# Four token mixers on one core: a thread weaver with decoupled stages, mixer operations at a priority of their own, and TensorE held to the order of emission

## The chip, the cores and the metric

The program runs on one core of a Trainium2 chip. The metric is device time in microseconds (us) of one execution. The kernel before takes 1378.37 us (median of 3 runs, 1376.46 to 1379.80). The engines are named as in the profile: PE is TensorE (matmul), PEld its weight load, DVE is VectorE, ACT is ScalarE, POOL is GpSimd, SP issues the DMAs.

## The reference

One layer over 2048 tokens of width 1024, in float32:

```
h    = rmsnorm(x) * pre_norm_w
proj = h @ w_in                       # 1024 x 3992, split in four groups
y    = [gated_deltanet(p_gdn),        # 4 heads of 64, chunks of 64 tokens, a triangular solve per chunk
        rwkv7(p_rwkv),                # 4 heads of 64, decayed state with a rank-one correction
        short_conv(p_sc),             # bg * conv3(cg * xv) * silu(z)
        gla(p_gla)]                   # 4 heads, key width 32, value width 64, chunks of 64
x    = x + rmsnorm(y @ w_out) * post_norm_w
```

Gated DeltaNet, RWKV7 and GLA each carry a state from chunk to chunk. The first two need, per chunk and head, the inverse of a 64x64 unit triangular matrix.

## The kernel before

Tokens go in 4 blocks of 512 (`NBLK`, `BL`), a block in 4 tiles of 128 (`TT`). For a block, `proj` multiplies h with one 128-channel tile of `w_in` at a time: weights and h are each split in a high and a low float32r part, so that a tile takes 24 matmuls of 512 columns (high x high, high x low, low x high, over 8 slices of the width) into one of two PSUM banks (`pp`). A function per tile takes the result out (`conv` for Gated DeltaNet, `mix` for RWKV7, and so on); its ACT and DVE operations carry a raised priority (`PRIO` 400), as do the split of the weights and the `hl` parts of the next block's h in `front` (`FPRIO` 400). GLA's value projection is the exception: `proj_v` has h as weights and `w_in` moving, in matmuls of 256 columns, and gives tokens by channels.

The mixers run as threads (Python generators) of one weaver, `weave`: `chains` (the recurrences, the state kept in SBUF), `inverses` (blockwise inversion: `Bb`, `W`, `X`, `Y`, `Yb`), `prepare` (gates, norms, decays, then the matrices of a pair of tiles in `gdn_mats` or `rwkv_mats`), `put` (outputs), `stats` (next block's h), `load_out`. The projections are the main thread. The weaver has a clock of its own: `mm` and `tr` add a planned cost, and a thread that yields a number from `LAT` is ready again that much later. Main runs for `BEAT` (1.5) planned us, which is two pieces of four matmuls, then all ready threads are stepped, again and again, until none is ready. Where neither can go on, the clock jumps. Threads also wait for each other's events: `prepare` begins the matrices of pair n when inverse n-1 is done ("I"), the inverses need the matrices ("B"), the chains the inverses.

That gives the order of emission. The order in which each engine executes is made afterwards, by a scheduler that takes the instructions of each engine by priority and readiness; TensorE's order is its choice too, and differs from the emission.

After the last projection, `out_proj` multiplies the four mixers' outputs (which went through DRAM, `yd`) with `w_out`; its weights are loaded by `load_out` once the last Gated DeltaNet tile is out, and 12 of its 16 token tiles need nothing of the last block.

Lines that the steps below touch: L595 `mmb`, L613 W and L618 X of the inverse, L605 the copy to the block diagonal `Yb`, L620 the transpose; L1005 and L1006 the DeltaNet chain's correction; L1064 and L1037 RWKV7's; L435 `hl` of the next block; L893 to L918 RWKV7's preparation; L1103 the normalised output. All matmuls have line L199, all transposes on TensorE L203.

Of the kernel before, what the change touches and what calls it, by code (L numbers as in the profile page):

```python
# [12 lines left out]
F16 = mybir.dt.float16  # L13
# [32 lines left out]
CST = {"ident": 0, "dlt": 128, "cum": 256, "msi": 384, "rst": 640, "bones": 640 + BL}  # L46
NCST = 640 + BL


def make_consts():  # L50
    c = np.zeros((P, NCST + P), np.float32)
    r = np.arange(P)
    blk = r[:, None] // 64 == r[None, :] // 64
    a, b = r[:, None] % 64, r[None, :] % 64
    c[:, 0:128] = np.eye(P)
    c[:, 128:256] = blk & (a > b)
    c[:, 256:384] = blk & (a <= b)
    j, i = r[:, None] % 64, np.arange(64)[None, :]

    c[:, 384:640] = np.concatenate([i > j, i >= j, i >= j, i > j], 1)  # L60
    c[:, 640:NCST] = np.arange(BL) % 64 > 0
    c[:, NCST:] = blk

    m = [j == i, -((j // 2 == i // 2) & (i % 2 == 1) & (j % 2 == 0)).astype(np.float32)]
    m += [-((j // (2 * s) == i // (2 * s)) & (j % (2 * s) >= s) & (i % (2 * s) < s)).astype(np.float32) for s in LEVELS]
    return c, np.concatenate([x.astype(np.float16) for x in m], 1)


def layout(inp):
# [4 lines left out]
    starts += [GLA0, GLA0 + 128, GLA0 + 512, GLA0 + 640]  # L74
# [5 lines left out]
    wv = w[:, GLA0 + 256:GLA0 + 512].reshape(KT, P, 256).transpose(1, 0, 2).reshape(P, KT * 256)  # L80
# [8 lines left out]
    for nm, key in (("w0", "rwkv_w0"), ("a0", "rwkv_a0"), ("kk", "rwkv_k_k"), ("ka", "rwkv_k_a"), ("rk", "rwkv_r_k"),  # L89
# [13 lines left out]
        "wv": wv,  # L103
# [24 lines left out]
class Ring:  # L128
# [6 lines left out]
    def __call__(self):  # L135
# [11 lines left out]
    "M4": (512, 4), "BKT": (512, 2), "UV": (512, 2),   # L147
    "ru": (256, 2), "lu": (256, 3), "or": (256, 2),  "Yf": (64 * 8, 1), "y": (256, 1),
    "t2": (BL, 4), "gk": (16, 9), "sx": (64, 1), "dr": (16, 1), "kn": (4 * TT, 3), "rB": (256, 1), "sm": (16, 14),

    "lqk": (BL, 2), "lv": (BL, 2), "lk": (128, 1), "lgz": (2 * BL, 1), "ld": (8, 1), "lg": (BL, 2), "n32": (32, 4), "gs": (TT, 2),
# [5 lines left out]
    "kq": (2 * BL, 2), "gv": (BL, 2), "ggz": (2 * BL, 1), "attn": (256, 2), "kT": (256, 4), "vT": (256, 2),  # L157
    "gu": (256, 3), "t1": (256, 3), "og": (256, 2), "gy": (256, 1),
}
RINGS16 = {"Bh": 1, "Bl": 1, "W": 1, "X": 2, "Y": 1}  # L160
# [7 lines left out]

BEAT = 1.5
# [3 lines left out]
LAT = {"gates": 6.0, "ipre": 2.0, "gates2": 1.0, "norms": 3.2, "chan": 0.9, "pool": 1.38, "decay": 2.6, "mats": 2.2, "inv0": 1.0, "inv1": 2.2,  # L173
       "invr": 0.8, "chA": 1.0, "chB": 0.7, "chC": 0.48, "rpre": 5.0, "rchan": 4.5, "gpre": 3.0, "gA": 1.1,
# [14 lines left out]

class K:  # L190
    def __init__(self, tc, a, out):
        self.tc, self.nc, self.a, self.out = tc, tc.nc, a, out
        self.t, self.left, self.ev, self.threads = 0.0, 0.0, {}, []


    def mm(self, out, w, x, **kw):
        n = math.prod(out.shape[1:])
        self.t += max(0.028, n * (1.67e-3 if w.dtype == F32 else 0.42e-3))
        return self.nc.tensor.matmul(out, w, x, **kw)  # L199

    def tr(self, out, x, ident):
        self.t += out.shape[1] * 0.83e-3
        return self.nc.tensor.transpose(out, x, ident)  # L203

    def thread(self, gen, prio):
        self.threads.append([prio, 0.0, None, gen])
# [12 lines left out]
    def step(self, th):  # L219
# [6 lines left out]
        else:  # L226
            th[1] = self.t + y

    def weave(self):
# [3 lines left out]
        while self.threads:  # L233
# [17 lines left out]
    def setup(self, ctx):  # L251
# [29 lines left out]
        self.rst = g("rst", BL)  # L281
        c16 = c.tile([P, 64 * (2 + len(LEVELS))], F16, name="c16")
# [187 lines left out]
    def load_half(self, blk, wi, i):  # L470
# [4 lines left out]
        if wi == "v":  # L475
            wh, wl = (t.rearrange("p (k c) -> p k c", k=2) for t in self.load_parts(blk, (wi, i), self.a["wv"][:, i * BL:(i + 1) * BL]))
            return (wh, self.hh), (wl, self.hh), (wh, self.hl)
# [3 lines left out]
    def proj(self, blk, groups):  # L481
# [3 lines left out]
        for n, (_, tiles, _) in enumerate(groups):  # L485
            nj = range(len(tiles))
            halves = [(n, j, i) for i in range(4 if tiles[0][0] == "v" else 2) for j in nj]
# [8 lines left out]
        for n, j, i, ks in work:  # L496
# [10 lines left out]
            if first:  # L507
                pss[n, j] = self.pp() if tiles[j][0] != "v" else [self.pp() for _ in range(2)]
# [3 lines left out]
            if tiles[j][0] == "v":  # L512
                yield from self.proj_v(ps, i, pairs)
                if i == 3:
                    with self.tc.high_priority(offset=PRIO):
                        tiles[j][1](ps)
                fin += 1
                continue
# [14 lines left out]
            yield 0.0  # L533

    def proj_v(self, ps, i, pairs):

        for q, (w, h) in enumerate(pairs):
            for k in range(2):
                for t in range(TT):
                    o = 256 * (t % 2)  # L540
                    self.mm(ps[t // 2][:, o:o + 256], h[:, 2 * i + k, t * P:(t + 1) * P], w[:, k, :], start=(i + q + k + t % 2 == 0),
                            stop=(i == 3 and q == 2 and k == 1), skip_group_check=True)
            yield 0.0
# [36 lines left out]
    def inverse(self, Bh, Bl, n):  # L580
# [9 lines left out]
        for c in range(2):  # L590
            nc.vector.tensor_copy(Bb[hs(c), :, hs(c)], Bh[hs(c)])
# [6 lines left out]
        nc.vector.tensor_tensor(Y, Bh, m4(self.n1t), ALU.mult)  # L598
        nc.vector.tensor_tensor(Y, Y, I16, ALU.add)
        X = self.R16["X"]()  # L600
        nc.vector.transpose(X, Y)
        def diag():
            Yb = self.Rbd["Yb"]()
            for c in range(2):
                nc.vector.tensor_copy(Yb[hs(c), :, hs(c)], Y[hs(c)])  # L605
# [3 lines left out]
        for lv in range(4):  # L609
# [3 lines left out]
            nc.vector.tensor_tensor(W, v(ps), m4(self.lev[lv]), ALU.mult)  # L613
# [4 lines left out]
            nc.vector.tensor_tensor(X2, v(ps), X, ALU.add)  # L618
            X = X2
            nc.vector.transpose(Y, X)  # L620
# [5 lines left out]
        nc.vector.tensor_tensor(W, v(ps), m4(self.lev[4]), ALU.mult)  # L626
# [8 lines left out]
        nc.vector.tensor_tensor(X2, v(px), X, ALU.add)  # L635
        nc.vector.tensor_tensor(Y, py, Y, ALU.add)
# [3 lines left out]
        nc.vector.tensor_tensor(T, I16, X, ALU.subtract)  # L640
# [8 lines left out]
        nc.vector.tensor_tensor(R, T, v(ps), ALU.subtract)  # L649
# [8 lines left out]
        nc.vector.tensor_tensor(v(Yf), v(ps), Y, ALU.add)  # L658
# [133 lines left out]
    def gdn_mats(self, tt, Bh, Bl):  # L792
# [10 lines left out]
        kT, vT = g["kT"][tt], self.R["vT"]()  # L803
        nc.vector.tensor_tensor(h4(kT), h4(kT), bc(g["ke"]), ALU.mult)
        ps = self.psa()
        for pr in range(2):
            self.tr(ps[:, pr * P:(pr + 1) * P], g["v"][pr][:, tt * P:(tt + 1) * P], self.ident)
        nc.vector.tensor_tensor(h4(vT), h4(ps[:, 0:256]), bc(g["kv"]), ALU.mult)
# [21 lines left out]
        return dict(attn=h4(attn), kT=kT, vT=vT)  # L830
# [38 lines left out]
    def rwkv_prep(self, blk):  # L869
# [10 lines left out]
        for pr in range(2):  # L880
# [15 lines left out]
            nc.scalar.activation(e[:, :, 1:65], c3(G), AF.Exp)  # L896
            ev = e.rearrange("p (a c) t -> p a c t", c=2)
            en, ak = self.t2(), self.t2()
            nc.scalar.activation(en, G, AF.Exp, scale=-1.0)
            kk = self.t2()  # L900
# [4 lines left out]
            nc.vector.tensor_tensor(slot(bks, 0), c4(ak), c4(en), ALU.mult)  # L905
            nc.scalar.activation(av, av, AF.Identity, scale=self.d[:, 17 + pr:18 + pr], bias=self.d[:, 13 + pr:14 + pr])
            nc.vector.tensor_tensor(k_, k_, m3(av), ALU.mult)
            nc.vector.scalar_tensor_tensor(m3(add[:, pr, :]), r_, self.pcol("rk", pr), k_, ALU.mult, ALU.mult)
            nc.vector.tensor_tensor(k_, k_, m3(en), ALU.mult)
# [39 lines left out]
    def rwkv_mats(self, tt, Bh, Bl):  # L949
# [22 lines left out]
        for pr in range(2):  # L972
            bd = BK[pr][:, 2 * tt:2 * tt + 2, :]
# [4 lines left out]
        for cp in range(2):  # L978
            for pr in range(2):
                o = (2 * cp + pr) * P  # L980
                self.tr(ps[:, o:o + P], BK[pr][:, 2 * tt + cp, :], self.ident)
# [478 lines left out]
```

## Time and profile before

| | |
|---|---|
| median of 3 runs | 1378.37 us |
| profiled execution | 1379.89 us, span 1378.1 us |
| TensorE busy | 1284.7 us (93%) |
| VectorE busy | 967.7 us (70%) |
| ScalarE, GpSimd busy | 530.2 us, 355.5 us |
| mean granted TensorE clock | 0.985 |
| DMA | 204.63 MB, mean 148 GB/s |

The chain of waits that ended last is TensorE almost throughout, so time is read from TensorE: what it executes, and where it stood still and for whom. The wait view gives for each waiting engine the operation that released it, total us, times, and the longest; the stretch view gives busy us of every engine in stretches of 50 us with the granted clock.

### The profile page before, as it was taken

The numbers are of one execution on the slowest core, as the hardware profiler recorded it, in microseconds if no ns is written. First come the engines' busy times: TensorE is split into PE (matmuls) and PEld (weight loads), VectorE is DVE, ScalarE is ACT, GpSimd is POOL, SyncE is SP. The second block draws the span as 40 slices with busy tenths as digits, with TensorE's granted clock in tenths as the row PEclk, the third lists the DMA queues.
The fourth block names the chain that finished last, engine by engine and source line by source line (L and its number), as shares of the span: only waits on it lengthen the run. The fifth ranks groups of instructions, "written<-read, shape, count | busy, mean of one in ns | idle before, by whom it ended". The sixth has DMA issues, their size and how long they took to land. (4 is left out here: it accounts for less than half of the span.)

```text
span 1378.1 us, 26007 instructions
## 1 busy us (share of the span) xinstructions
PE 1284.7 (93%) x10088; PEld 982.1 (71%) x10088; DVE 967.7 (70%) x2194; ACT 530.2 (38%) x1167; POOL 355.5 (26%) x437
## 2 busy tenths in 40 slices
PE   5989988899999999999999999999998998999997
PEld 3767766767667767767777677776776776677886
DVE  5766698869876895778657977888669847743232
ACT  4663454336242431425423432453224325133221
POOL 5554444201221021101301210203111135233321
PEclk9999999999999999999999999999999999999999
DMA  8776554544244424453543335432444363233442
GB/s 283 263 258 231 206 177 146 177 152 133 82 139 146 157 89 135 146 177 105 173 146 130 130 120 174 144 110 68 127 143 145 103 198 121 89 99 116 151 151 100
DMA packets 98509, 204.63 MB, mean 148 GB/s; under 512 B 9153, under 2 KB 39249, under 8 KB 98385
## 3 DMA queue, kind: packets, MB, share of 16 engines
q1 hardware_dynamic: 98384, 202.96, 44.6%
q8 instruction: 79, 1.29, 0.4%
q14 instruction: 46, 0.37, 0.1%
HBM read 153.65 MB, written 49.28 MB: 147 GB/s over the span
## 5 line engine op out<-in xcount | busy, mean ns | idle before, releaser
L199 PE MATMUL pp<-hh,w 128*128 128x512 f32 (+1 forms) x2144 | 609.6, 408 | 7.6 <-DMA w<-parts 5.9
L199 PEld LDWEIGHTS pp<-hh,w 128*128 128x128 f32 (+1 forms) x2144 | 389.8, 190 | 92.0 <-issue 4.7
L199 PE MATMUL pp<-hl,w 128*128 128x512 f32 (+1 forms) x1088 | 323.1, 408 | 2.0 <-POOL hl L435 2.0
L199 PEld LDWEIGHTS pp<-hl,w 128*128 128x128 f32 (+1 forms) x1088 | 198.2, 190 | 45.4 <-POOL hl L435 3.8
L352 POOL TENSOR_TENSOR w<-raw,w 128x512 fp32r<-128x512 f32 (+1 forms) x102 | 129.3, 1270 | 223.6 <-ACT w L351 143.0
L351 ACT CAST w<-raw 128x512 fp32r<-128x512 f32 (+1 forms) x102 | 60.3, 593 | 130.5 <-issue 56.8
L356 POOL TENSOR_TENSOR sm<-sm,mhalf 128x4 f32<-128x4 f32 (+1 forms) x64 | 59.3, 927 | 193.4 <-DVE sm L1099 148.7
L199 PE MATMUL pp<-woh,w 128*128 128x512 f32 x256 | 71.8, 401 | 0.0
L681 DVE SCALAR_TENSOR_TENSOR pq<-pq,par,pq 128x512 f32<-128x512 f32 x72 | 59.4, 826 | 11.0 <-ACT pq L678 8.5
L605 DVE COPY Yb<-Y 64x512 f16<-64x512 f16 x160 | 55.8, 349 | 2.2
L199 PEld LDWEIGHTS <-Yb 128*128 128x128 f16 x640 | 25.2, 98 | 41.5 <-issue 22.9
L199 PEld LDWEIGHTS pp<-woh,w 128*128 128x128 f32 x256 | 47.6, 191 | 9.7
L199 PE MATMUL psi<-W,Yb 128*128 128x64 f16 x640 | 32.7, 194 | 22.3 <-DVE W L613 17.5
L618 DVE TENSOR_TENSOR X<-psi,X 128x512 f16<-128x512 f32 x64 | 43.9, 686 | 12.8 <-PE psi L199 12.5
L199 PEld LDWEIGHTS <-Bb 128*128 128x128 f16 x768 | 29.8, 99 | 29.5 <-issue 23.4
L613 DVE TENSOR_TENSOR W<-psi,c 128x512 f16<-128x512 f32 x64 | 43.8, 685 | 5.9 <-PE psi L199 5.3
L1393 DVE SCALAR_TENSOR_TENSOR pq<-pq,sm,x 128x512 f32<-128x512 f32 x32 | 24.6, 769 | 30.4 <-DMA x<-in_x 19.7
L620 DVE STREAM_TRANSPOSE Y<-X 128x512 f16<-128x512 f16 x64 | 45.2, 707 | 0.7
L199 PE MATMUL psi<-X,Bb 128*128 128x64 f16 x768 | 40.0, 195 | 6.2 <-DVE X L618 4.2
L1382 ACT ACTIVATE x<-pp 128x512 f32<-128x512 f32 x32 | 19.1, 598 | 64.1 <-PE pp L199 64.1
L847 ACT COPY pq<-pp 128x512 f32<-128x512 f32 x36 | 21.1, 586 | 53.0 <-PE pp L199 53.0
L199 PE MATMUL pp<-w,hh 128*128 128x256 f32 x256 | 36.6, 289 | 0.1
(320 smaller groups left out, 2152.4 us busy)
## 6 DMA issues: line engine op xcount, KB each, us to landing
w<-parts SPq DMA_DIRECT2D x174, 512.0 KB, 3.3
parts<-w SPq DMA_DIRECT2D x58, 512.0 KB, 4.0
raw<-in_wt SPq DMA_DIRECT2D x58, 256.0 KB, 3.2
x<-in_x SPq DMA_DIRECT2D x56, 256.0 KB, 3.0
raw<-yd SPq DMA_DIRECT2D x32, 256.0 KB, 2.9
out<-pq SPq DMA_DIRECT2D x32, 256.0 KB, 2.0
x<-in_xt SPq DMA_DIRECT2D x24, 256.0 KB, 2.9
w<-parts_v SPq DMA_DIRECT2D x12, 512.0 KB, 3.3
```

The costliest lines, as they stand in the source:

```text
L199: return self.nc.tensor.matmul(out, w, x, **kw)
L351: self.nc.scalar.copy(hi, src)
L352: self.nc.gpsimd.tensor_tensor(lo, src, hi.bitcast(F32), ALU.subtract)
L356: self.nc.gpsimd.tensor_tensor(dst, x, self.mhalf[:, 0:x.shape[1]], ALU.pow)
L605: nc.vector.tensor_copy(Yb[hs(c), :, hs(c)], Y[hs(c)])
L613: nc.vector.tensor_tensor(W, v(ps), m4(self.lev[lv]), ALU.mult)
L618: nc.vector.tensor_tensor(X2, v(ps), X, ALU.add)
L620: nc.vector.transpose(Y, X)
L681: nc.vector.scalar_tensor_tensor(acc, p[:, i:i + BL], self.pcol("conv", 4 * ct + i), acc, ALU.mult, ALU.add)
L847: nc.scalar.copy(p[:, 1:], ps)
L1382: nc.scalar.activation(junk, ps[i], AF.Square, accum_out=ss[:, i:i + 1])
L1393: nc.vector.scalar_tensor_tensor(o, o, r, x, ALU.mult, ALU.add)
```

## The change

Six things change together.

1. **One step per visit.** A thread that yields a positive number is stepped once in a visit; before, a visit went on until no thread was ready.
2. **Order held.** `mm` and `tr` tie each TensorE instruction to the one emitted before it, so TensorE executes in the order of emission.
3. **Priority.** The inverse's and the chains' operations on DVE and ACT go through wrappers (`self.uv`, `self.ua`) at a priority of 800 (`URGENT`), above the 400 of the projections.
4. **Decoupled stages.** `prepare` may be two pairs ahead of the inverses (`Bh` and `Bl` get two buffers, `M4` six, `attn` three). `gdn_mats` and `rwkv_mats` give up what the inverse doesn't need to `gdn_more` and `rwkv_more`, which run after the matrices; the chains wait for them ("M").
5. **Preparations in pieces.** `rwkv_prep` and `gla_prep` yield two or three times more (`rpre` 5.0 becomes 1.0 and three `burst` of 0.5). To pay for the buffers, `rwkv_prep` reuses `add` and `lw` (`t2` 4 to 3), `BKT` goes (the transposes are copied back into `BK`), `gy` is merged with `y`, `rst` becomes float16.
6. **v by channel.** GLA's v is projected like every other tile, in two tiles, and each token tile's v is transposed on TensorE in `gla` and copied out together with `ke`.

```diff
 class K:
     def mm(self, out, w, x, **kw):
         n = math.prod(out.shape[1:])
         self.t += max(0.028, n * (1.67e-3 if w.dtype == F32 else 0.42e-3))
-        return self.nc.tensor.matmul(out, w, x, **kw)
+        return self.after(self.nc.tensor.matmul(out, w, x, **kw))
...
+    def after(self, ins):
+        if self.prev is not None:
+            info = mybir.DependencyInfo(mybir.DependencyClass.NoSync, mybir.DependencyReason.DATA)
+            self.tc.add_manual_dep(ins.ins, self.prev.ins.name, info, reason="order of emission")
+        self.prev = ins
+        return ins
...
+class Urgent:
+    def __getattr__(self, name):
+        op = getattr(self.eng, name)
+        def f(*a, **kw):
+            with self.tc.high_priority(offset=URGENT):
+                return op(*a, **kw)
+        return f
...
             elif ready:
+                self.visit += 1
                 while ready:
                     for th in ready:
                         self.step(th)
-                    ready = [th for th in self.threads if th[0] < 99 and self.can(th)]
+                    ready = [th for th in self.threads if th[0] < 99 and self.can(th) and th[4] < self.visit]
...
-        todo += [(None, (("v", fv),), None)]
+        ... for i, t in enumerate([qf, kf] + v)]
...
-            nc.vector.tensor_tensor(W, v(ps), m4(self.lev[lv]), ALU.mult)
+            self.uv.tensor_tensor(W, v(ps), m4(self.lev[lv]), ALU.mult)
...
-                    if n:
-                        yield "I", n - 1
+                    if n > 1:
+                        yield "I", n - 2
...
+                    self.done("B", n, lat=LAT["mats"])
+                    for i in range(2):
                         if pair:
                             yield "T", name, blk, i
-                        m = yield from (self.gdn_mats if name == "G" else self.rwkv_mats)(...)
-                        ms.append(m)
-                    self.mats[n] = ms, B
-                    self.done("B", n, lat=LAT["mats"])
+                        yield from more(2 * pair + i, ms[i])
+                    self.done("M", n, lat=LAT["more"])
...
-        self.tr(pt[:, 0:P], L["ed"][:, ts], self.ident)
-        nc.scalar.copy(ke, pt[:, 0:P])
+        for i, t in enumerate([L["ed"]] + L["v"]):
+            self.tr(pt[:, i * P:(i + 1) * P], t[:, ts], self.ident)
+        self.ua.copy(kv, pt[:, 0:3 * P])
```

The order in which the instructions stand changes at these places. First VectorE at the end of the first block, where the next block's `hl` is made while an inverse runs. Before:

```order
L605 COPY Yb_153<-Y_150 64x8x64 x2
L435 TENSOR_TENSOR hl<-x_143,hh 128x512
L435 TENSOR_TENSOR hl<-x_144,hh 128x512
L613 TENSOR_TENSOR W_147<-psi,c_203 128x512
L428 SCALAR_TENSOR_TENSOR x_143<-x_143,par,E_71 128x512
L618 TENSOR_TENSOR X_148<-psi,X_149 128x512
```

And now (L201 is the wrapper's line, L463 the line of `hl`):

```order
L201 COPY Yb_153<-Y_151 64x8x64 x2
L201 TENSOR_TENSOR Sr<-Sr,dr_102 128x256
L201 TENSOR_TENSOR W_148<-psi,c_204 128x512
L456 SCALAR_TENSOR_TENSOR x_142<-x_142,par,E_71 128x512
L571 SCALAR_TENSOR_TENSOR lgz_126<-pq_137,pq_136 128x512
L201 TENSOR_TENSOR UV_79<-psc,kn_105 64x2x64
L201 TENSOR_TENSOR UV_79<-psc,kn_104 64x2x64
L201 TENSOR_TENSOR X_150<-psi,X_149 128x512
L463 TENSOR_TENSOR hl<-x_142,hh 128x512
```

W stood behind two `hl` operations; now the inverse and a chain stand together, and `hl` behind them. From the first to the last of the eight `hl` there are 30, 41 and 26 rows at the three block ends before, and 54, 45 and 45 now.

Next TensorE at the end of the projections, where the last inverse (psi) meets the first matmuls with `w_out` (woh, wol). Before, with repeated rows left out:

```order
L199 MATMUL psi<-X_149,Bb_151 128x64
...
L199 MATMUL pp<-hh,w_159 128x512 x4
...
L199 MATMUL psi<-W_147,Yb_153 128x64
...
L199 MATMUL pp<-hl,w_159 128x512 x4
L199 MATMUL pp<-hh,w_159 128x512
...
L199 MATMUL psi<-X_148,Bb_151 128x64
...
L199 MATMUL pp<-hh,w_159 128x512 x3
L199 MATMUL pp<-hh,w_160 128x512 x3
```

And now:

```order
L215 MATMUL psi<-W_148,Yb_154 128x64
...
L215 MATMUL psi<-X_149,Bb_152 128x64
...
L215 MATMUL psi<-W_148,Yb_153 128x64
...
L215 MATMUL psi<-X_150,Bb_152 128x64
...
L215 MATMUL psi<-W_148,Yb_154 128x64
...
L215 MATMUL psa<-Y_151,W_148 64x64
...
L219 MATMUL psa<-cst,or_86 128x128 x2
...
L215 MATMUL pp<-woh,w_160 128x512 x4
```

Before, some matmuls of a projection stood between any two steps of the inverse; now two levels follow each other with nothing between, and soon after them seven steps of RWKV7's chain with next to nothing. Elsewhere it is the other way round: counted over the whole order, between a step of an inverse or of a DeltaNet or RWKV7 chain and the step whose result it takes there were fewer than 8 projection matmuls of 512 columns (or as many columns in smaller ones) in 117 of 377 places before, and are in 15 of 365 now, 12 of these with none at all. The projections' matmuls (w_in and w_out) stood in 448 unbroken groups and stand in 364.

## Rows read from the trace of the kernel before

**Rows 1.** The page: busy time of each engine, share of the span, instructions.

```profile
PE 1284.7 (93%) x10088; PEld 982.1 (71%) x10088; DVE 967.7 (70%) x2194; ACT 530.2 (38%) x1167; POOL 355.5 (26%) x437
```

**Rows 2.** PE's waits: line, releaser: total us, times, longest us.

```profile
PE psi L199 <- DVE W L613: 17.5, 17, 4.8
PE psa L203 <- POOL gs L356: 11.5, 1, 11.5
PE psc L199 <- DVE gu L1006: 8.2, 16, 1.2
...
PE psi L199 <- DVE X L618: 4.2, 5, 2.1
...
PE psa L203 <- DVE or L1103: 4.0, 3, 3.0
PE psa L199 <- DVE t L801: 3.5, 1, 3.5
PE psi L199 <- DVE Yb L605: 2.5, 4, 0.9
PE psc L199 <- DVE Sg L1037: 2.4, 6, 0.9
...
PE psi L199 <- DVE W L626: 2.1, 3, 1.0
...
PE psa L203 <- ACT t L901: 0.2, 1, 0.2
```

**Rows 3.** Timeline, DVE, 180 to 189 us: start, us, what.

```profile
182.60 2.77 DVE L605 COPY Yb<-Y 64x512 f16<-64x512 f16 x2
...
186.00 1.22 DVE L893 TENSOR_TENSOR_SCAN t<-cst,t 128x512 f32<-128x512 f32 x1
187.15 0.68 DVE L613 TENSOR_TENSOR W<-psi,c 128x512 f16<-128x512 f32 x1
```

**Rows 4.** Timeline, PE, 178 to 189 us.

```profile
187.88 0.58 PE L199 MATMUL psi<-W,Yb 128*128 128x64 f16 x8 [4.78 <-DVE W L613]
```

**Rows 5.** Timeline, DVE and then PE, 262 to 266 us.

```profile
262.55 2.27 DVE L435 TENSOR_TENSOR hl<-x,hh 128x512 fp32r<-128x512 f32 x2
...
265.47 0.39 PE L199 MATMUL psi<-W,Yb 128*128 128x64 f16 x8 [0.87 <-DVE W L613]
```

**Rows 6.** Stretches: PE, PEld, DVE, ACT, POOL busy, PEclk, DMA share, GB/s.

```profile
50.00:100.00 50.00, 44.68 (x221) 35.42 (x220) 36.46 (x82) 33.11 (x74) 26.08 (x29) 0.90 0.72 249
150.00:200.00 50.00, 44.66 (x286) 33.51 (x285) 41.54 (x80) 25.01 (x46) 25.38 (x24) 0.93 0.51 180
450.00:500.00 50.00, 46.76 (x359) 35.48 (x358) 46.05 (x98) 27.09 (x53) 8.98 (x11) 1.00 0.39 125
1150.00:1200.00 50.00, 43.99 (x375) 31.84 (x375) 38.19 (x73) 16.23 (x36) 20.05 (x18) 0.97 0.32 102
```

**Rows 7.** Chain that ended last: start us, us, what.

```profile
1217.18 2.05 PE pp L199 x8
...
1220.07 1.85 PE pp L199 x8
...
1273.60 97.06 PE pp L199 x428
```

**Rows 8.** PE's groups: busy us, mean ns, then idle before.

```profile
L199 PE MATMUL pp<-hh,w 128*128 128x512 f32 (+1 forms) x2144 | 609.6, 408 | 7.6 <-DMA w<-parts 5.9 <-ACT hh L434 1.6
...
L199 PE MATMUL pp<-w,hh 128*128 128x256 f32 x256 | 36.6, 289 | 0.1
...
L199 PE MATMUL pp<-w,hl 128*128 128x256 f32 x128 | 18.6, 288 | 0.0
...
L203 PE MATMUL psa<-cst,rv 128*128 128x128 f32 x32 | 7.0, 280 | 0.3 <-DVE M L964 0.3
```

**Rows 9.** DVE's groups of the inverse.

```profile
L605 DVE COPY Yb<-Y 64x512 f16<-64x512 f16 x160 | 55.8, 349 | 2.2
L620 DVE STREAM_TRANSPOSE Y<-X 128x512 f16<-128x512 f16 x64 | 45.2, 707 | 0.7
...
L613 DVE TENSOR_TENSOR W<-psi,c 128x512 f16<-128x512 f32 x64 | 43.8, 685 | 5.9 <-PE psi L199 5.3
```

More of the change, by code (lines that the diff above doesn't have):

```diff
@@ L73, in layout @@
     starts += [SC0 + P * i for i in range(8)]
-    starts += [GLA0, GLA0 + 128, GLA0 + 512, GLA0 + 640]
+    starts += [GLA0 + P * i for i in range(6)]
     tiles = [w[:, s:s + P].reshape(KT, P, P).transpose(1, 0, 2).reshape(P, KT * P) for s in starts]
@@ L167 @@
 FPRIO = 400
+URGENT = 800
 BEAT = 1.5
@@ L227, in step @@
             th[1] = self.t + y
+            if y > 0.0:
+                th[4] = self.visit
     def weave(self):
@@ L486, in proj @@
             nj = range(len(tiles))
-            halves = [(n, j, i) for i in range(4 if tiles[0][0] == "v" else 2) for j in nj]
+            halves = [(n, j, i) for i in range(2) for j in nj]
             order += halves
@@ L507, in proj @@
             if first:
-                pss[n, j] = self.pp() if tiles[j][0] != "v" else [self.pp() for _ in range(2)]
+                pss[n, j] = self.pp()
             if n == 0:
@@ L829, in gdn_mats, with gdn_more @@
         nc.gpsimd.tensor_tensor(Bl, h4(B32), Bh, ALU.subtract)
-        return dict(attn=h4(attn), kT=kT, vT=vT)
+        return dict(attn=h4(attn))
+    def gdn_more(self, tt, m):
+        nc = self.nc
+        g = self.g
+        bc = lambda s: s[:, 4 * tt:4 * tt + 4].unsqueeze(2).to_broadcast([P, 4, 64])
+        kT, vT = g["kT"][tt], self.R["vT"]()
+        nc.vector.tensor_tensor(h4(kT), h4(kT), bc(g["ke"]), ALU.mult)
+        ps = self.psa()
+        for pr in range(2):
+            self.tr(ps[:, pr * P:(pr + 1) * P], g["v"][pr][:, tt * P:(tt + 1) * P], self.ident)
+        nc.vector.tensor_tensor(h4(vT), h4(ps[:, 0:256]), bc(g["kv"]), ALU.mult)
+        m.update(kT=kT, vT=vT)
+        yield 0.0
     def rwkv_proj(self):
@@ L971, in rwkv_mats, with rwkv_more @@
         nc.gpsimd.tensor_tensor(Bl, h4(B32), Bh, ALU.subtract)
-        for pr in range(2):
-            bd = BK[pr][:, 2 * tt:2 * tt + 2, :]
+        yield 0.0
+        return dict(M4=M4)
+    def rwkv_more(self, tt, m):
+        nc = self.nc
+        r = self.r
+        BK = r["BK"]
+        bds = [BK[pr][:, 2 * tt:2 * tt + 2, :] for pr in range(2)]
+        for pr, bd in enumerate(bds):
             for c in range(2):
@@ L977, in rwkv_mats @@
         ps = self.psa()
[L978 to L981, printed above, removed]
-        bt = self.R["BKT"]()
-        nc.scalar.copy(bt, ps)
+        for pr, bd in enumerate(bds):
+            for cp in range(2):
+                o = (2 * pr + cp) * P
+                self.tr(ps[:, o:o + P], bd[:, cp], self.ident)
+        for pr, bd in enumerate(bds):
+            nc.scalar.copy(bd, ps[:, 2 * P * pr:2 * P * pr + 2 * P].rearrange("p (c x) -> p c x", c=2))
         ps = self.psa()
@@ L1145, in prepare @@
                 for pair in range(TT // 2):
-                    if n:
-                        yield "I", n - 1
+                    if n > 1:
+                        yield "I", n - 2
                     B, ms = [self.R16[x]() for x in ("Bh", "Bl")], []
+                    mats, more = (self.gdn_mats, self.gdn_more) if name == "G" else (self.rwkv_mats, self.rwkv_more)
+                    for i in range(2):
+                        tt = 2 * pair + i
+                        if tt == 3:
+                            yield "T", name, blk, 0
+                        m = yield from mats(tt, *(t[:, 4 * i:4 * i + 4, :] for t in B))
+                        ms.append(m)
+                    self.mats[n] = ms, B
+                    self.done("B", n, lat=LAT["mats"])
                     for i in range(2):
@@ L1313, in gla @@
         o = u1()
-        nc.scalar.copy(o, po[:, 0:256])
+        self.ua.copy(o, po[:, 0:256])
         self.norm(o, u1, EPS, False)
```

143 lines of the change are left out of this document (60 added, 83 removed).

## The prediction

> **What bounds the kernel now.** First the page's busy times: TensorE works 1284.7 of a span of 1378.1 us, VectorE 967.7 [rows 1]. So TensorE sets the pace, 93.4 us of the span have no matmul in them, and VectorE is the engine on which the rest hangs. What TensorE has to compute hardly changes; the question is how much of the 93.4 us goes, and what the new order loses elsewhere.
>
> Second, TensorE's waits. 11.5 us are the wait for the first norm, at the start, which the change doesn't touch. The mixers' waits are what it aims at: 17.5 for the inverse's W, 8.2 for DeltaNet's correction, 4.2, 4.0, 3.5, 2.5 and 2.4, together 42.3, and 18 smaller entries from 2.1 down to 0.2, together 17.1 [rows 2]. That makes 59.4 us, nearly all behind VectorE. What remains of the 93.4 is the end after the last matmul, waits for weights, h and gates.
>
> Third, why W is late. The longest wait, 4.78 us, stands at 187.9 [rows 4]. On VectorE, W itself takes 0.68; ahead of it went two copies drawn out to 2.77 and an RWKV7 scan of 1.22, which no inverse waits for [rows 3]. At the first block end two `hl` operations take 2.27 us right ahead of W, and TensorE waits 0.87 [rows 5]. So the waits are VectorE's queue order more than its total. Only more: in some stretches VectorE is busy 46.05 of 50 us while TensorE has 46.76 [rows 6]. There a better order moves a wait rather than removes it.
>
> Fourth, the granted clock. Most stretches have 1.00, but 50 to 100 us has 0.90 and 150 to 200 has 0.93 [rows 6]; the second contains the 4.78 us wait [rows 4], and 1150 to 1200, one of six stretches at 0.97, has TensorE idle for 6.0 us [rows 6]. [...]
>
> [...]
>
> **The change, part by part**, against the profiled execution's 1379.9 us (span 1378.1 and 1.8 outside it).
>
> *One step per visit, and order held.* Now all but 15 of 365 steps have 8 projection matmuls or more ahead of them, 1.85 us or 2.05 [rows 7], where 117 of 377 had fewer. W needs 0.685, X and the transpose about 0.7 each [rows 9], so 1.85 us hide one of them and one foreign operation of some 0.8. *Priority* puts W right behind its own copies rather than behind `hl` or a scan. Bounds: nothing of the 59.4 us goes (VectorE's total is unchanged, and busy stretches stay busy), or all of it. The waits inside 1150 to 1200, 6.0 us of the 50 [rows 6], I treat below, which leaves 53.4. I take 60%: most waits have one or two foreign operations as their cause, as rows 3 and 5 show, but the stretches with VectorE at 46 of 50 keep theirs. **-32.**
>
> *Fewer breaks.* 364 groups of projection matmuls instead of 448. Eight matmuls take 2.05 us behind a group of small mixer matmuls and 1.85 behind a transpose [rows 7]; at the rate of the long unbroken run, 97.06 / 428 x 8, they take 1.81. A break costs 0.04 to 0.24 us, 84 fewer give 3 to 20. I take 0.12: **-10.**
>
> *Clock.* [...] If three fifths of the waits go, some of the drops stay, and the gates' and start's waits aren't touched: **-6.**
>
> *v by channel.* Out: 36.6 + 18.6 = 55.2 us of 256-column matmuls [rows 8]. In: 8 tiles of 24, 192 x 609.6/2144 = 54.6. Also in: 32 transposes of 128 columns for v, for which RWKV7's 32 took 7.0 us busy [rows 8]; they stand behind another transpose of the same group, so less of them may show. The copy out grows from 128 to 384 columns on ScalarE, which has 848 us free. **+5** (bounds +3 and +7).
>
> *The end of the projections.* In the held order the last inverse's two levels have nothing between their steps. A level on VectorE is X, transpose, two copies, W: 0.69 + 0.71 + 0.70 + 0.69 = 2.8 us [rows 9], of which TensorE fills 0.8 with its own two steps of 0.4: 2 x 2.0 = 4. Then three more operations of 0.7 for the closing step, 2, and some five uncovered steps of RWKV7's chain, not less than half of a W each and not more than a whole one, 1.7 to 3.5. Sum 7.7 to 9.5. The same place loses 6.0 us now [rows 6]: **+3** (bounds +1 and +12, the upper one if the first weights of `w_out` come late as well).
>
> *The block ends.* `hl` now lies behind the mixers' operations: from first to last there are 144 rows on VectorE at three block ends instead of 97. At the mean of 967.7/2194 = 0.44 us [rows 1], 47 rows are 21 us by which the next block's h is finished later. TensorE has mixers' steps of its own there and needs the first slices first: **+5** (bounds 0 and +21).
>
> *Decoupling and pieces.* Same instructions; earlier matrices let an inverse run beside the chain of the pair before, so the mixers' steps come in common groups (the 84 breaks fewer). It also packs more of VectorE's work into the same time; that is the upper bound of the first part. Only three `t2` instead of four tie the two halves of `rwkv_prep` closer together; nothing on TensorE waits for them now beyond 0.2 us, by the last row of the waits [rows 2]. 0.
>
> Sum: -32 -10 -6 +5 +3 +5 = -35. 1379.9 - 35 = 1344.9 profiled; the median shown lies 1.5 lower, which gives **1343 us**. The remaining uncertainty of the first term alone, 40 to 85% of 53.4, is 1330 to 1354; with the others, the likeliest case's own range is 1320 to 1364.
>
> **Rivals.**
>
> *All waits go.* If priority and spacing empty the whole list: -53 -17 -14 +3 +1 +0 = -80, so 1298. For it: nearly every wait names VectorE, and VectorE has 410 us free over the span. Against it: 46 of 50 busy where the mixers overlap.
>
> *VectorE is the bound.* Where inverse and chain run side by side, a level (2.8 us) and the chain's operations compete with the projections' own 0.8 us operations, and TensorE waits for PSUM or `hl` instead of for W. Then a quarter of the waits goes: -13 -10 -2 +5 +3 +10 = -7, 1371. For it: rows 6, third row. Against it: the average, 70%.
>
> *Slower: a late operand now stops everything.* TensorE can't be given another order by the scheduler any more, and VectorE executes its own in the order given, an urgent operation that waits for a matmul holding back the projections' results behind it. Place: the three block ends and the end of the projections. Price: 21 + 12 + 7 for transposes, and the rest of the waits only changes its place, with 10 us won and the breaks' saving of 3: +27, 1405. It decides once less than about 40 us is won by the first three parts together, so already from a third of the mixers' waits.
>
> [...]
>
> *The order does nothing.* That the waits come from VectorE's total and neither priority nor spacing matters, while the costs above are small: within 0.2%. That is the narrow strip between the two rivals before.
>
> **Chances.** Forecast 0.54; all waits go 0.12; VectorE the bound 0.16; slower 0.14; nothing 0.04. The range of 8 in 10 runs from 1302 to 1384: it holds the forecast, most of the second case and of the third, and cuts half of the slower one. 0.2% is 2.8 us, about what a measurement of this kernel can tell from no change, so faster means below 1375.6. Forecast, all waits, and three quarters of the third case are faster: 0.78. Within: 0.06. Slower: 0.16.
>
> **What the profile after would show.** The wait for W falls from 17.5 to below 7, that for DeltaNet's correction from 8.2 to below 2; VectorE's busy time stays at 960 to 975 and its share rises to 72%; TensorE's busy time rises or falls by no more than 15 us; one cluster of waits of 8 to 12 us appears around the first w_out matmuls, with psi and psc steps in it; at the block ends waits of pp for `hl` appear, of 2 us each or less; the granted clock is 0.99. Wrong would be: waits of pp for ScalarE or VectorE that sum to over 20 us, a wait for W still above 12, or a busy TensorE below 1260, which would mean that much of what counts as busy is waiting.

## The result and the profile after

The changed kernel takes 1464.19 us (median of 4 runs, 1462.09 to 1465.25), the kernel before 1377.41 us beside it (1370.01 to 1379.80): a ratio of 1.063, 95% interval [1.0605, 1.0657]. The forecast was 1343 and faster.

The profiled execution has a span of 1461.4 us, 83.3 more than before. The page, busy time by engine:

```profile
PE 1306.4 (89%) x9928; PEld 994.6 (68%) x9928; DVE 972.3 (67%) x2194; ACT 532.4 (36%) x1181; POOL 357.4 (24%) x437
```

Against [rows 1], VectorE, ScalarE and GpSimd do what they did, to 5 us. TensorE is busy 21.7 us longer and idle 1461.4 - 1306.4 = 155.0 us instead of 93.4, so 61.6 of the 83.3 us are idle time. Who it waits for (line, releaser: total us, times, longest; L201 is the wrapper's line):

```profile
PE psc L215 <- DVE gu L201: 17.6, 18, 2.2
PE psa L215 <- DVE t L809: 15.1, 5, 3.7
PE psi L215 <- DVE X L201: 14.0, 8, 4.5
PE psa L219 <- POOL gs L384: 12.1, 1, 12.1
PE psi L215 <- DVE W L201: 9.1, 18, 1.8
PE pp L215 <- ACT hh L462: 8.7, 8, 2.8
PE psa L215 <- DVE AR L928: 8.6, 4, 2.4
PE psa L215 <- DVE sm L1117: 7.4, 2, 3.7
PE psa L219 <- DVE attn L829: 7.1, 8, 4.4
PE psa L215 <- DVE M L982: 6.9, 4, 2.2
PE psa L215 <- DVE gk L736: 6.2, 2, 3.9
```

W, the first row of [rows 2], fell from 17.5 to 9.1. Instead the correction (`gu`) rose from 8.2 to 17.6, `t` of DeltaNet's matrices from 3.5 to 15.1, and steps stand in the list that had no entry or a small one: the gates' product (`sm`, `gk`), RWKV7's `AR` and `M`, DeltaNet's `attn`. The 7.4 us under `sm` belong to the gates' product as well (its operand is `gk`; the profile names the VectorE operation that ended last, one of the outputs' norm), which had 4.0 us before. The waits are spread over many operands, not held by one.

Two of these places, PE's timeline (start us, us, what, [idle before <-releaser]):

```profile
364.64 1.08 PE L215 MATMUL pp<-hh,w 128*128 128x512 f32 x4
365.65 0.45 PE L215 MATMUL psc<-ru,Yf 64*64 64x64 f32 x8
369.98 1.35 PE L215 MATMUL psa<-gk,cst 128*128 128x16 f32 x6 [3.88 <-DVE gk L736]
...
371.93 2.08 PE L215 MATMUL pp<-hh,w 128*128 128x512 f32 x4
...
525.00 2.07 PE L215 MATMUL psa<-AR,BK 64*128 64x128 f32 x14 [2.39 <-DVE AR L928]
529.25 2.07 PE L215 MATMUL psa<-AR,BK 64*128 64x128 f32 x14 [2.18 <-DVE M L982]
```

At 366 TensorE stands for 3.88 us before the gates' product of the next tiles, though the projection matmuls behind it need nothing from it: they are executed right after it. Then four of them take 2.08 us where four took 1.08 just before: the granted clock is 1.00 through the wait, 0.51 in 370 to 372 us and 0.50 in 372 to 376, and these four matmuls alone add 1.00 us to the 3.88 of the wait. The stretches that answer to [rows 6]:

```profile
50.00:100.00 50.00, 41.73 (x212) 32.82 (x211) 36.33 (x80) 33.03 (x74) 27.92 (x31) 0.90 0.71 243
...
500.00:550.00 50.00, 43.07 (x330) 33.41 (x329) 46.42 (x99) 24.30 (x52) 10.11 (x10) 0.90 0.32 102
...
1200.00:1250.00 50.00, 34.33 (x329) 26.59 (x328) 38.54 (x69) 19.75 (x43) 27.48 (x23) 0.84 0.46 145
```

Only 6 of the first 26 stretches have 1.00, where 18 had before. The clock records of both traces have two values, 1.00 and 0.50 (24 records of each after, 10 of each before), so the time at the lower one is 2 x (1 - mean clock) x span: 2 x 0.049 x 1461.4 = 143 us after, 2 x 0.015 x 1378.1 = 41 before. If matmuls at 0.50 last twice as long, an estimate from the 2.08 and 1.08 us above, the extra 102 us would have been 51 at the least at 1.00, had all of it been matmuls; part of it was waiting, so 51 is an upper bound of the clock's share. TensorE's busy time grew by 21.7 us, less than that.

### The profile page after: what moved, and what is told of

Read it like the earlier page. It is cut to its first block, busy times and chain, and to the rows that moved or that the text cites. A ratio compares the mean times of both kernels' runs of the same rounds, so it can differ in the third digit from the quotient of the medians.

```text
span 1461.4 us, 25697 instructions
## 1 busy us (share of the span) xinstructions
PE 1306.4 (89%) x9928; PEld 994.6 (68%) x9928; DVE 972.3 (67%) x2194; ACT 532.4 (36%) x1181; POOL 357.4 (24%) x437
## 4 chain that ended last, share of the span: by engine, by line
PE 54%; DVE 30%; issue 5%; DMA 4%; ACT 3%; POOL 3%; SPq 0%; ACTq 0%; POOLq 0%; DVEq 0%
PE pp L215 40%; PE psc L215 6%; PE psa L215 4%; DVE gu L201 3%; DVE Y L201 2%; PE psi L215 2%; DVE X L201 2%; DVE Yb L201 2%; PE psa L219 2%; DVE W L201 2%; POOL sm L384 1%; DVE Sg L201 1%; DMA x<-in_xt 1%; DVE pq L689 1%; DVE x L456 1%
## 5 line engine op out<-in xcount | busy, mean ns | idle before, releaser
L215 PE MATMUL pp<-hh,w 128*128 128x512 f32 (+1 forms) x2272 | 644.3, 414 | 10.7 <-ACT hh L462 8.7
L215 PEld LDWEIGHTS pp<-hh,w 128*128 128x128 f32 (+1 forms) x2272 | 423.9, 194 | 106.1 <-ACT hh L462 10.1
L215 PE MATMUL pp<-hl,w 128*128 128x512 f32 (+1 forms) x1152 | 339.1, 411 | 2.7 <-POOL hl L463 1.5
L215 PEld LDWEIGHTS pp<-hl,w 128*128 128x128 f32 (+1 forms) x1152 | 211.8, 192 | 51.2 <-DVE hl L463 3.8
L384 POOL TENSOR_TENSOR sm<-sm,mhalf 128x4 f32<-128x4 f32 (+1 forms) x64 | 61.6, 962 | 258.5 <-DVE sm L1124 234.9
L201 DVE TENSOR_TENSOR W<-psi,c 128x512 f16<-128x512 f32 x80 | 54.8, 685 | 15.4 <-PE psi L215 14.2
L201 DVE TENSOR_TENSOR X<-psi,X 128x512 f16<-128x512 f32 x80 | 54.9, 686 | 10.8 <-PE psi L215 10.2
L201 DVE COPY Yb<-Y 64x512 f16<-64x512 f16 x160 | 56.5, 353 | 1.8
L863 ACT COPY pq<-pp 128x512 f32<-128x512 f32 x36 | 21.2, 588 | 94.0 <-PE pp L215 94.0
L215 PE MATMUL psa<-AR,BK 64*128 64x128 f32 x256 | 31.2, 357 | 19.1 <-DVE AR L928 8.6
L1426 DVE SCALAR_TENSOR_TENSOR pq<-pq,sm,x 128x512 f32<-128x512 f32 x32 | 24.1, 755 | 34.2 <-DMA x<-in_x 23.6
L201 DVE STREAM_TRANSPOSE Y<-X 128x512 f16<-128x512 f16 x64 | 45.0, 703 | 0.4
L215 PEld LDWEIGHTS psa<-AR,BK 64*128 64x128 f32 x256 | 25.5, 248 | 25.3 <-DVE AR L928 9.5
```

The source lines that it names most:

```text
L201: return op(*a, **kw)
L215: return self.after(self.nc.tensor.matmul(out, w, x, **kw))
L384: self.nc.gpsimd.tensor_tensor(dst, x, self.mhalf[:, 0:x.shape[1]], ALU.pow)
L863: nc.scalar.copy(p[:, 1:], ps)
L1426: nc.vector.scalar_tensor_tensor(o, o, r, x, ALU.mult, ALU.add)
```

## The experiments

### The order held, alone and taken away

To the kernel before only the tie is added (`o_hold`); from the changed one only the tie is taken (`u_hold`).

```diff
-        return self.nc.tensor.matmul(out, w, x, **kw)              # o_hold; tr in the same way
+        return self.after(self.nc.tensor.matmul(out, w, x, **kw))
...
-        if self.prev is not None:                                  # u_hold
+        if False:
```

> The kernel before with TensorE tied to the order of emission and nothing else. Theory A (the held order is the greater part of the loss by itself): 1420 to 1450 us, TensorE idle 125 to 150 us, clock 0.95 to 0.965. Rival (the held order only hurts together with the new emission, its burst of matrices and its early preparations): 1370 to 1400.

> The changed kernel with the tie between TensorE's instructions taken out; emission, priorities and everything else as changed. Theory A (the held order is the cost: TensorE stops at each operand that is later than the planner thought, and nothing may be moved into the gap): 1340 to 1400 us, TensorE's waits down from 155 us idle to below 110. Theory B (the priority of 800 starves the preparations that TensorE needs next): little change, 1440 to 1470, since the same operations on VectorE are still put last. Theory C (the emission itself is bad: matrices are emitted too soon after their preparation and four at once for three banks): 1400 to 1440, the scheduler repairs a part.

`o_hold`: 1461.82 us, ratio 1.0628 [1.0578, 1.0678], clock 0.950. `u_hold`: 1403.12, 1.0187 [1.0134, 1.024], clock 0.979. So the tie on the old kernel makes the whole loss, 85 us, where 1420 to 1450 was expected; the five other edits, on top of the tie, make none (1464 against 1462), and without it they still cost 25 us. `u_hold` lies just above the range of theory A (the order) and within that of theory C (the emission): taking the tie out wins back 61 us, not all. In `o_hold` TensorE executes the same 10088 matmuls as before: it is busy 1307.2 us instead of 1284.7 and idle 153.9 instead of 93.4, so 60.5 of the 83.0 us by which the span grew are idle time. The waits in `o_hold` (its lines are 7 higher than before's):

```profile
PE psi L199 <- DVE W L620: 44.3, 24, 5.4
PE psa L203 <- POOL gs L363: 12.8, 1, 12.8
PE psc L199 <- DVE UV L1071: 12.7, 12, 1.9
PE psc L199 <- DVE gu L1013: 11.7, 12, 1.8
```

The wait for W is 44.3 us where it was 17.5 [rows 2]. The gates' place of above in `u_hold`:

```profile
356.10 0.45 PE L215 MATMUL psc<-ru,Yf 64*64 64x64 f32 x8
356.48 1.19 PE L215 MATMUL pp<-hh,w 128*128 128x512 f32 x4
357.52 1.08 PE L215 MATMUL pp<-hl,w 128*128 128x512 f32 x4
358.52 0.45 PE L215 MATMUL psc<-UV,BK 128*64 128x64 f32 x8
358.81 0.64 PE L215 MATMUL psc<-UV,M 128*64 128x64 f32 x16
359.37 1.66 PE L215 MATMUL pp<-hh,w 128*128 128x512 f32 x6
361.38 0.84 PE L215 MATMUL psa<-gk,cst 128*128 128x16 f32 x6 [0.34 <-DVE gk L736]
```

After the same `ru` product, fourteen projection matmuls and two steps of the chain now stand ahead of the gates' product, and the wait is 0.34 instead of 3.88.

### Which freedom the tie takes

Three weaker ties on the kernel before. In `o_two` projection matmuls (main thread) are tied to each other and the mixers' instructions to each other, with nothing between the two chains. `o_mafter` adds: no mixer step ahead of a projection matmul emitted before it. `o_pafter` adds the reverse: no projection matmul ahead of a mixer step emitted before it.

```diff
+        tie(self.last[self.main])
+        if not self.main:          # o_mafter; o_pafter: if self.main: tie(self.last[False])
+            tie(self.last[True])
```

> The kernel before with the order held in two chains: every projection matmul behind the projection matmul emitted before it, every other TensorE instruction behind the other one emitted before it, with no tie from one chain to the other. Theory A (the loss of the held order is that the scheduler can no longer move projection matmuls against the mixers' steps): the two chains stay free against each other, so 1370 to 1390, wait for W below 15. Theory B (the order of the mixers' steps among themselves is what costs): 1440 to 1465.

> As two chains, and each mixer instruction is also tied behind the last projection matmul emitted before it: projections may be drawn ahead of a mixer's step, the step never ahead of them. Theory A1 (a step whose operand is late is passed by later projection matmuls): 1370 to 1395, as with two chains. Theory A2 (the scheduler gains by taking a ready step earlier than emitted): 1430 to 1465.

> As two chains, and each projection matmul is also tied behind the last mixer instruction emitted before it: a mixer's step may be drawn ahead, projections may not pass a step that waits. Theory A1 (a late step must be passed): nearly all of the loss, 1440 to 1465, wait for W above 30. Theory A2: 1370 to 1400.

| | us | ratio | idle | clock |
|---|---|---|---|---|
| `o_two` | 1382.15 | 1.0035 [1.001, 1.006] | 102.9 | 0.983 |
| `o_mafter` | 1381.42 | 1.0028 [0.9997, 1.006] | 107.2 | 0.983 |
| `o_pafter` | 1458.46 | 1.0582 [1.0519, 1.0645] | 151.6 | 0.954 |
| `o_hold` | 1461.82 | 1.0628 [1.0578, 1.0678] | 153.9 | 0.950 |

(Idle is span minus TensorE's busy time in the profiled execution.) The order of the mixers' steps among themselves and their being drawn ahead of projections are worth some 4 us together (`o_mafter`, whose interval includes no change); as it carries at least as many ties as `o_hold`, the ties themselves aren't what costs. What carries is one direction: a projection matmul that is ready may pass a mixer step that isn't. Theory A1 holds, with nearly the whole loss in `o_pafter`. (Only W's wait was higher than expected in `o_two`, 23.3 us where under 15 was expected.) The clearest place is RWKV7's chain in the first block end. PE's timeline in `o_mafter`:

```profile
369.13 0.63 PE L199 MATMUL pp<-hh,w 128*128 128x512 f32 x2
370.05 0.45 PE L199 MATMUL psc<-ru,Yf 64*64 64x64 f32 x8 [0.29 <-ACT ru L1067]
370.43 1.43 PE L199 MATMUL pp<-hh,w 128*128 128x512 f32 x5
373.52 0.45 PE L199 MATMUL psc<-UV,BKT 128*64 128x64 f32 x8 [1.66 <-DVE UV L1075]
```

and in `o_pafter`:

```profile
374.72 0.69 PE L199 MATMUL psc<-ru,Yf 64*64 64x64 f32 x8
377.28 0.70 PE L199 MATMUL psc<-UV,BKT 128*64 128x64 f32 x8 [1.87 <-DVE UV L1075]
...
386.53 1.23 PE L199 MATMUL psc<-Sr,AR 128*128 128x128 f32 x4 [2.38 <-DVE Sr L1048]
388.22 0.69 PE L199 MATMUL psc<-ru,Yf 64*64 64x64 f32 x8 [0.46 <-ACT ru L1067]
```

The old weaver steps the chain again and again until none is ready, so it emits it in one piece. Where projections may pass, they lie between the steps; where they may not, the chain runs alone, waits at nearly every step, and the same eight `ru` matmuls take 0.69 us instead of 0.45: the page of `o_pafter` has a granted clock of 0.7 in its slice from 364 to 400 us, where that of `o_mafter` has 0.9 or more from 346 to 380.

### More planned distance

If late operands are the loss, later steps might cure it. `LAT` for the steps of the inverse and the chain's first step is raised to 2.7 us, nearly the 2.8 that a level takes on VectorE [rows 9], in `o_hold` (`o_hold_lat`) and in the changed kernel (`u_lat`).

```diff
-"inv0": 1.0, "inv1": 2.2, ... "chA": 1.0
+"inv0": 2.7, "inv1": 2.7, ... "chA": 2.7
```

> The kernel before with the held order, and with longer planned times for the handovers that wait most there: inv0 1.0 to 2.7, inv1 2.2 to 2.7, chA 1.0 to 2.7, so that the planner puts 16 instead of 8 matmuls before the inverse's W and DeltaNet's correction. If the held order costs because 8 matmuls (1.85 us) are too few wherever VectorE's queue is long: the wait for W falls from 44.3 to below 12, that for the correction from 11.7 to below 5, time 1405 to 1435. If the held order costs by something else (the mere sequence, LDWEIGHTS, the clock by itself): 1450 or more, and the waits only move.

> The changed kernel with the same longer planned times. Its waits stand less at W (9.1) and more at the correction (17.6), at t (15.1), X (14.0) and the preparations, so the same cure reaches less: 1435 to 1455. If only the handovers of inverse and chain mattered: 1410 to 1430.

`o_hold_lat` takes 1488.54 us, ratio 1.081 [1.0729, 1.089], and `u_lat` 1481.57, 1.0759 [1.0666, 1.0851]: both worse. The first came out as its second expectation had it, the other lies above both of its ranges. Waits of `o_hold_lat`:

```profile
PE psc L199 <- DVE UV L1071: 19.4, 17, 4.1
PE psi L199 <- DVE Yb L612: 16.4, 10, 2.2
PE psi L199 <- DVE W L620: 15.6, 9, 4.8
PE psi L199 <- DVE X L625: 15.0, 17, 1.6
```

W did fall from 44.3 to 15.6, though not below 12, and others rose; TensorE's idle time went from 153.9 to 169.0 us. One stretch, first of `o_hold` and then of `o_hold_lat`, tells why (columns as in [rows 6]):

```profile
1000.00:1050.00 50.00, 46.39 (x499) 34.61 (x500) 31.82 (x81) 14.06 (x36) 10.56 (x16) 0.83 0.26 80
```

```profile
1000.00:1050.00 50.00, 32.29 (x382) 24.06 (x380) 35.88 (x110) 8.50 (x24) 5.97 (x8) 0.66 0.08 25
```

In this stretch `o_hold` executes 83 projection matmuls of hh and hl; in `o_hold_lat` it is 15, all in the first 4 us, and TensorE runs mixers' steps alone for the rest. At the first block end it is the same: from 100 to 200 us `o_hold_lat` executes 357 of them against 292 in `o_hold`, and from 375 to 425 none against 35. A block has a fixed number of projection matmuls to put between the steps; what a longer distance spends early is missing at the block's end.

### The other edits, alone and taken away

Each alone on the kernel before: the priority (`o_urgent`), v by channel (`o_v`, with one ring for the two outputs to make room), one step per visit (`o_step`).

```diff
+                    ready = [th for th in self.threads if th[0] < 99 and self.can(th) and th[4] < self.visit]   # o_step
+            nc.vector... -> self.uv..., nc.scalar... -> self.ua...                                              # o_urgent
+    starts += [GLA0 + P * i for i in range(6)]                                                                  # o_v
```

> The kernel before with the priority of 800 for the mixers' operations alone; order free, emission as before. If the priority is what costs the 25 us that the changed kernel keeps without the held order: 1390 to 1405. If it is the emission: 1365 to 1380, with the wait for the inverse's W down from 17.5 to below 10.

> The kernel before with v by channel alone (and one buffer for the DeltaNet and the other outputs, to make room). If v costs a part of the 25 us: 1385 to 1395. By the prediction's term of +5: 1380 to 1386.

> The kernel before with one step per visit alone, TensorE's order free. If the emission rule costs a part of the 14 us that are left without held order and priority: 1383 to 1395. If the scheduler evens it out: 1372 to 1382.

1378.38 (1.0022 [1.0002, 1.0043]), 1379.87 (1.0008 [0.9977, 1.0038]) and 1375.37 (0.9988 [0.9962, 1.0015]): none moves the time by more than 0.22%. In `o_urgent` W's wait falls from 17.5 to 10.4 us, and the time stays. Each taken from the changed kernel, with the tie left in: the priority (`u_urgent`), the visit rule (`u_step`), the pieces (`u_prep`).

```diff
-            with self.tc.high_priority(offset=URGENT):
-                return op(*a, **kw)
+            return op(*a, **kw)                                    # u_urgent
-"rpre": 1.0, "burst": 0.5
+"rpre": 5.0, "burst": 0.0                                          # u_prep
```

> The changed kernel with the wrappers giving no priority. Theory A: 1450 to 1480, the waits for the inverse's W and the chains grow, those for the preparations shrink, the sum stays. Theory B: 1380 to 1410. Theory C: within 15 us of 1464.

> The changed kernel with the old rule for a visit (threads are stepped until none is ready). Theory A: slower still or the same, 1460 to 1500, since held steps have less between them. Theory B and C: within 20 us of 1464, the waits at the preparations stay.

> The changed kernel with the planned time of RWKV7's preparation put back (rpre 5.0 at the place where it stands, burst 0), so that what follows is emitted later. Theory A: 1440 to 1460, only RWKV7's share of the waits goes (8.6 for AR, 6.9 for M, 5.6 for t). Theory B: as A. Theory C: 1410 to 1440.

1450.46 (1.0531 [1.0481, 1.058]), 1461.34 (1.061 [1.0557, 1.0662]) and 1460.23 (1.0602 [1.0554, 1.0649]): only the first is clear of the changed kernel's 1.0631. Without the priority W's wait is 34.2 us instead of 9.1, and yet the kernel is 14 us faster: the priority moved the wait from W to other operands, and under the held order these stop the engine too. In `u_prep` the wait for `AR` falls from 8.6 to 2.2, and a new one of 23.4 for `t` of RWKV7's preparation appears.

### What costs on the free order

From the changed kernel: without tie and priority (`u_hu`); without the visit rule too (`u_hus`); then also with the planned times of the preparations' yields as before (`u_husp`), with `prepare` only one pair ahead again (`u_nodec`, whose edit is shown), or with both (`u_nodecp`).

```diff
-                    if n > 1:
-                        yield "I", n - 2
+                    if n:
+                        yield "I", n - 1
```

> The changed kernel without the held order and without the priority: left are one step per visit, decoupling, pieces and v. If the priority costs: 1375 to 1395. If the emission costs: 1400 to 1420, the wait for W back at 15 or more.

> The changed kernel without held order, priority and the rule for visits: decoupling, pieces and v by channel are left. If these cost the 14 us: 1385 to 1395, with the wait for the inverse's first step (X out of Y, 25.8 with the rule) still over 15. If the rule does: 1372 to 1382.

> The changed kernel without the held order, the priority and the visit rule (1399.6 before), and with the preparations' yields as before (rpre 5.0, burst 0): decoupled stages and v by channel are left. If the pieces make the 20 us: 1378 to 1386. If the decoupling makes them: 1394 to 1402.

> The changed kernel without held order, priority and visit rule, and with prepare again allowed only one pair ahead of the inverses; the split preparations, the M event, the reused buffers and v by channel stay. If being two pairs ahead makes the 16 to 22 us that are left: 1378 to 1386. If it is the split of the matrices and the pieces: 1392 to 1400.

> As u_nodec, and the yields of the preparations as before too. What is left of the change are gdn_more and rwkv_more behind the matrices, the M event, the reused buffers and v by channel. If two pairs ahead and the pieces make the loss: 1376 to 1382. If the split of the matrices or the reused buffers make it: 1390 to 1397.

| | us | ratio | clock |
|---|---|---|---|
| `u_hu` | 1391.71 | 1.0119 [1.0072, 1.0165] | 0.981 |
| `u_hus` | 1399.57 | 1.0163 [1.0099, 1.0227] | 0.977 |
| `u_husp` | 1394.28 | 1.0116 [1.0057, 1.0176] | 0.979 |
| `u_nodec` | 1377.29 | 0.9995 [0.9972, 1.0019] | 0.990 |
| `u_nodecp` | 1366.76 | 0.9924 [0.9896, 0.9952] | 0.992 |

Two pairs ahead costs 22 us (`u_hus` to `u_nodec`) or 28 (`u_husp` to `u_nodecp`), clear of the intervals both times. The pieces cost 11 us one pair ahead (`u_nodec` to `u_nodecp`); two pairs ahead their 5 us (`u_hus` to `u_husp`) lie within the intervals, and so do the 11 us that the priority seems to cost here (`u_hold` to `u_hu`) and the 8 by which the kernel gets slower when the visit rule is taken out (`u_hu` to `u_hus`). What is left in `u_nodecp`, the matrices split into what the inverse needs and the rest, the changed buffers and v by channel, is 0.8% faster than the kernel before, and so the fastest of all; neither expectation had that. Since v by channel alone is neutral, the split or the buffers probably make the gain, but neither was run alone. Its wait for W is 21.2 us, more than the 17.5 of the kernel before.

One place where two pairs ahead costs is the second block end. `u_husp` and `u_nodecp` each execute 32 products of `AR` there, those of one pair of tiles. The stretches that hold most of them, `u_husp` and then `u_nodecp`, columns as in [rows 6]:

```profile
500.00:510.00 10.00, 9.41 (x72) 7.34 (x72) 8.05 (x24) 4.00 (x10) 1.45 (x3) 0.57 0.00 1
```

```profile
480.00:490.00 10.00, 8.83 (x109) 6.85 (x109) 9.86 (x24) 3.67 (x8) 3.54 (x4) 1.00 0.40 133
```

PE's timeline in `u_husp`:

```profile
498.73 0.41 PE L214 MATMUL psi<-W,Yb 128*128 128x64 f16 x8 [0.57 <-DVE Yb L200]
499.06 1.16 PE L214 MATMUL psa<-AR,BK 64*128 64x128 f32 x8
500.81 0.39 PE L214 MATMUL psi<-X,Bb 128*128 128x64 f16 x8 [0.59 <-DVE X L200]
...
501.50 2.07 PE L214 MATMUL psa<-AR,BK 64*128 64x128 f32 x8
...
503.69 0.79 PE L214 MATMUL pp<-hl,w 128*128 128x512 f32 x1
504.42 1.86 PE L214 MATMUL psa<-AR,BK 64*128 64x128 f32 x9
```

and in `u_nodecp`:

```profile
487.27 0.50 PE L214 MATMUL psa<-S,bones 128*128 128x512 f32 x1 [0.26 <-POOL S L379]
487.70 1.59 PE L214 MATMUL psa<-AR,BK 64*128 64x128 f32 x12
489.23 0.44 PE L214 MATMUL psi<-Y,W 64*64 64x64 f16 x16
489.60 1.38 PE L214 MATMUL psa<-AR,BK 64*128 64x128 f32 x12
490.90 0.73 PE L214 MATMUL pp<-hh,w 128*128 128x512 f32 x2
```

In `u_husp` the granted clock is 1.00 in 490 to 500 us and 0.57 on average in 500 to 510, which at the two values 1.00 and 0.50 puts the fall at about 501.4: eight `AR` matmuls take 1.16 us at 499.06 and 2.07 at 501.50. From 497.1 on no projection matmul had been executed, and TensorE had stood still twice, for 0.57 and 0.59 us. Most of the 9.41 busy us lie behind the fall, at the longer durations. In `u_nodecp` no projection matmul is executed from 485.8 to 490.9 either, 24 of the products stand there, and the clock stays at 1.00 (480 to 500 us); TensorE stood still once, for 0.26 us. So a bundle of small matmuls alone doesn't explain the fall. The gaps differ between these rows, but that they made the fall isn't shown.

Nor does the clock explain all of the 28 us. By the same estimate as above, from the mean clocks, `u_husp` spends 59 us at the lower level and `u_nodecp` 22; the 37 between them cost at most half, 18 us. TensorE's idle time is 98.0 against 89.9. Where the rest goes, and why two pairs ahead brings it, stays open.

## Why the prediction was wrong

- **The failed step** is "One step per visit, and order held", -32. It counted steps with fewer than 8 projection matmuls ahead, 117 before and 15 after, and took 1.85 us for each as cover. Planned distance is not what hid the waits. The old kernel had a second cover that the count doesn't see: the scheduler put later projections ahead of whichever step was late. Holding the order takes that away, for +85 us alone (`o_hold`), +80 in the one direction that matters (`o_pafter`). The 59.4 us of waits [rows 2], of which the step counted on 32, were what that cover had left over, not what there was to gain: TensorE's idle time rose by 61.6 us.
- **Priority** did at W what was said, under the tie (34.2 to 9.1 us), and the time rose by 14: the wait was not "VectorE's queue order more than its total", it moved. The prediction's own remark on the row of [rows 6] with VectorE at 46.05 of 50 us, that a better order there moves a wait, held far beyond that row.
- **Clock**, -6 (-17 in the first rival): wrong in sign. That fewer waits give clock back was the author's estimate, and no run shows the term. What the runs show: (1 - 0.985) x 1378.1 = 21 us of full clock not granted in the whole span before and 0.049 x 1461.4 = 72 after, or 41 and 143 us at the lower level.
- **Fewer breaks**, -10: not seen. hh and hl matmuls take 414 and 411 ns on average, where both took 408 (hh in [rows 8]); what fewer breaks may have saved can't be told apart from what the lower clock cost.
- **v by channel**, +5 (+3 to +7): alone it is +0.08% [-0.23, 0.38], which is -3 to +5 us: a cost can't be told from noise, nor the lower half of the term ruled out. The 32 new transposes take 6.1 us busy.
- **End of the projections**, +3 (+1 to +12): 1200 to 1250 us has 15.7 us idle where the place had 6.0, so +9.7. The mechanism was right (`X`, `Yb` and W in turn, up to 3.8 us each, 12.3 together, and 2.9 at RWKV7's chain), the size within its bounds but three times the +3.
- **Block ends**, +5: the waits for `hl` stayed under 2 us each (2.7 together), but `hh` on ScalarE cost 8.7, and the burst of `AR` products 15.5 with `M`.
- **Decoupling and pieces**, 0: two pairs ahead cost 22 to 28 us on the free order and the pieces 11 one pair ahead. The step took "same instructions" for "same time"; why the time differs is open, as told above.

Of the signs named ahead, VectorE's busy time (972.3) and `hl` came true. The correction's wait (17.6, not below 2), TensorE's busy time (21.7 more, not within 15) and the clock (0.951, not 0.99) did not; W at 9.1 lay between "below 7" and "above 12". No condition for "wrong" was met, though the forecast was wrong: these conditions looked at W, at the projections' own waits and at TensorE's busy time, and the new waits came at other steps. The slower rival, "a late operand now stops everything", had the mechanism on TensorE. (That VectorE executes in the order given shows at one place of the trace before: the product that `X` takes ended at 265.86 us, VectorE stood idle for 1.55 us until an `x` ahead of it had its load, and `X` began at 267.63. What this cost after the change was not measured.) The rival was placed only at the block ends and the end of the projections and priced at 1405, with "the rest of the waits only changes its place": that is the part mis-sized, since the rest grew instead.

After the 3.88 us wait the granted clock was 0.51 (370 to 372 us), and four matmuls took 2.08 us instead of 1.08. In `u_husp` the clock fell at about 501 us with no gap over 0.6 us in the 16 us before; what brought that fall about no run here shows.

## What to carry over

Read a wait list as what is left after the scheduler's work, and before pinning an engine's order ask what passes a late instruction today: here ready matmuls of an independent stream, worth 80 us, while the order within each stream was worth next to nothing. The wait for one operand is no measure of the time: the fastest kernel waits 21.2 us for W, the one before 17.5. If order has to be held, hold it within a stream and leave the independent stream free against it. Work moved earlier isn't free, even with the same instructions: two pairs ahead cost 22 to 28 us where the order was free.

## What the runs showed of the hardware

- A gap of 3.88 us was followed by four 512-column matmuls in 2.08 us instead of 1.08, at a granted clock of 0.50 instead of 1.00: the lower clock shows in the durations right behind the gap.
- A high busy share stood beside a low clock: TensorE was busy 9.41 of 10 us at a mean clock of 0.57 (`u_husp`, 500 to 510 us) and 8.83 of 10 at 1.00 (`u_nodecp`, 480 to 490). In the first, eight `AR` matmuls took 2.07 us, where eight had taken 1.16 just before the fall: the longer matmuls count as busy.
- With the same 10088 matmuls, the time at the lower clock, estimated from the mean clock as above, went from 41 us (before) to 241 (`o_hold_lat`, 2 x 0.081 x 1489.8) by the order of instructions alone.
